# Forgetting attention in a two-block kernel: sum and row extreme in one VectorE operation, P divided on ScalarE, S5's output stored by SyncE

## The chip, the cores and the metric

The kernel runs on one core of one Trainium2 chip. Its engines are TensorE (PE in the profile), VectorE (DVE), ScalarE (ACT), GpSimd (POOL) and SyncE (SP, which issues DMAs). The metric is the device time of one execution in microseconds; three runs of the kernel before took 1682.77, 1688.86 and 1692.17 us, median 1688.86.

## What is computed

Two blocks act one after the other on x, 512 positions by 1024 channels, in float32. The first has a state-space branch, a gated linear recurrence and an attention to a memory; the second, with which the change deals, has forgetting attention (12 heads of 64), an S5 state-space layer (768 channels in 48 groups, state 64) and an attention to a memory. Cut to the two parts that matter:

```python
# forgetting attention; log_f = log_sigmoid(fl + b_forget), F = cumsum(log_f)
s = q @ k.T / sqrt(64) + F[t] - F[s]      # for s <= t, else -1e30
out = softmax(s) @ v                      # then * silu(gf)
# S5: a complex diagonal state driven by u, with a scan over the positions
h[t] = a * h[t-1] + B @ u[t];  y[t] = Re(C @ h[t]) + D * u[t]   # then gelu, gates
```

Softmax does not change when a number is added to a whole row, so the kernel leaves F[t] out and adds only -F[s].

## The kernel before

**Tiling.** The positions are 4 blocks of 128. Every matrix product is done in float32r from a high and a low part of both factors. A weight is loaded by SP in pieces of 512 KB (`wraw`, three buffers), its high part is a ScalarE copy (`whi`, L267), its low part a VectorE subtraction (`wlo`, L280), five buffers each. The unit of TensorE's main work is a *share*: half of such a job, 12 matmuls of 128x512. A job of two shares ends with an evacuation of its PSUM tile.

**Order.** All engines execute in the order in which the program is written. `lay` puts named steps between the shares by hand: in a plan string, `t12@7` puts the step t12 ahead of share 7, and steps with the same number stand in the string's order. A share itself first issues the weight splits for shares up to four ahead, then the callbacks put off with `after`, then its matmuls, then (if odd) its evacuation.

**The six turns.** `window(j, ...)` handles heads 2j and 2j+1 and one S5 block. For j below 5, its ten shares are those of the next turn's u, k, v, q and gf, in this order; the plan is `WINDOW` (L1740). The last turn has 16 shares and `LAST_WINDOW` (L1743). The steps, with a the head and tt the block of query rows:

- `s`a tt (L1679): two matmuls give the scores of 128 queries against n = 128(tt+1) keys. VectorE writes P = 0.125 scores + nb, in one operation for the n-128 earlier keys (L1691, nb = -F[s] broadcast to all partitions) and in one for the diagonal block (L1692, nbm, the same with -1e30 above the diagonal), then takes the negated row maximum (L1693). ScalarE takes the exponential with that bias and sums the rows (L1694).
- `n`a tt (L1696): VectorE takes the reciprocal of the row sums (L1699) and multiplies P (L1700).
- `t`a tt (L1702): TensorE transposes P block by block (L1708), ScalarE copies the result to SBUF (L1710). `pv` multiplies by v.
- `vt` (L1659): transposes of v, whose evacuation is L1325.
- `M0`, `M1` (L1670): for the next turn's head 0 or 1, SP loads nb (L1672) and GpSimd makes nbm (L1674).
- `nb`, `wc` (L1482, L1494): GpSimd prepares the next turn's S5 coefficients; nb ends with a sign change of 128 columns on VectorE (L1491), wc with the powers `vt` and `rho` (L1513).
- `kk`, `kt`, `tg`, `ld`, `u`: S5's kernel matrix, its copies to `Tg` by SP (L1545), the coefficients and u for the next turn, loaded by SP (L1452, L1459).
- `S`, `R`, `y`: states by matmul; the recurrence on VectorE (L1567 to L1584, reading the powers); the output by TensorE (L1592, L1596), copied by ScalarE (L1599) and stored in eight DMAs that ScalarE issues (L1601).

After the k job's evacuation, the next share splits k: ScalarE copies (L1639), VectorE subtracts (L1641), SP copies each to the other half of the partitions (L1640, L1642). In `WINDOW`, share 4 does that. The steps ahead of shares 5, 6 and 7 are nb, y; then t10, t11, n12, n13, M1; then t12, t13. Ahead of the turns, the first turn's own k, v, q, gf stand with u, `fox_nb` and `fox_vt` between them (L1768).

Of the kernel before, what the change touches and what calls it, by code (L numbers as in the profile page):

```python
# [10 lines left out]
AF = mybir.ActivationFunctionType  # L11
ALU = mybir.AluOpType
AX = mybir.AxisListType
# [6 lines left out]
EPS = 1e-6  # L20
WSPLIT = 5
NEG = -1e30


class Cols:
# [146 lines left out]
def two_blocks(ctx, tc, A, out):  # L172
    nc = tc.nc
    V, S, G, PE, SP = nc.vector, nc.scalar, nc.gpsimd, nc.tensor, nc.sync
# [51 lines left out]
    def lay(fillers, plan, steps):  # L226

        fl = []
        for f in fillers:
            fl.extend([(f, i) for i in range(len(f.parts))] if isinstance(f, Job) else [f])  # L230
        at = [(w.split("@")[0], int(w.split("@")[1])) for w in plan.split()]
        for i in range(len(fl) + 1):
            prog.extend(steps[n] for n, p in at if p == i or (i == len(fl) and p > i))
            if i < len(fl):
                prog.append(fl[i])
# [67 lines left out]
    ones = const.tile([128, 128], F32, name="ones")  # L303
# [32 lines left out]
    def ph2(name):  # L336
        o, n = P2.at[name]
        return p2[:, o:o + n]
# [17 lines left out]
    def xtile():  # L356
        return psx.tile([128, 512], F32, tag="x", name="x")
# [4 lines left out]
    def scr():  # L362
        return sp.tile([128, 512], F32, tag="t", name="t", bufs=8)

    def wide(t):
        return t.rearrange("p c h -> p (c h)")
# [110 lines left out]
    def pt(pool, tag, shape=(128, 512), dt=F32, bufs=1):  # L477
        return pools[pool + "_"].tile(list(shape), dt, tag=tag, name=tag, bufs=bufs)
# [245 lines left out]
    def q_job(j):  # L724
        def ev(ps):
            qt[j].extend(hp_tile("mrg", 2 * (j % 4) + z, F32R) for z in range(2))
            split_to(*qt[j], ps)
        return gemm(A["w_in"][WI["q"] + j], H, ev)
# [36 lines left out]
    q = [q_job(j) for j in range(8)]  # L765
# [258 lines left out]
    def ssd_step(g, what):  # L1024
# [48 lines left out]
        def l():  # L1073

            j = i
            for q_ in range(2):
                h = hs + 2 * j + q_
                M = R["M"][2 * j + q_] = pt("ssp", "M", (128, 4, 128), bufs=6)
                SP.dma_start(wide(M), acs_d[h].partition_broadcast(128))
                G.affine_select(M, M, [[0, 4], [1, 128]], ALU.is_ge, NEG, base=0, channel_multiplier=-1)  # L1080

# [237 lines left out]
    def norm2(dst, ps, scale=1.0):  # L1319

        r2 = nrm["r2"][:ps.shape[0]]
        if scale == 1.0:
            V.tensor_tensor(dst, ps, r2, ALU.mult)
        else:
            V.scalar_tensor_tensor(dst, ps, scale, r2, ALU.mult, ALU.mult)  # L1325
# [24 lines left out]
    y_d = dram.tile([768, 8, 64], F32, name="y_d")  # L1350
    s5 = {}

    def cmul(o, a, b, x, y):

        G.tensor_tensor(x, a[0], b[1], ALU.mult)
        G.tensor_tensor(y, a[1], b[1], ALU.mult)
        G.tensor_tensor(o[1], a[1], b[0], ALU.mult)
        G.tensor_tensor(o[0], a[0], b[0], ALU.mult)
        G.tensor_tensor(o[1], o[1], x, ALU.add)
        G.tensor_tensor(o[0], o[0], y, ALU.subtract)  # L1360
# [102 lines left out]
    def q4(i):  # L1463
        return s5["bc"][:, 64 * i:64 * i + 64].rearrange("p (a h) -> p a h", a=4)

    def s5_xy():
        return pt("s5p", "x"), pt("s5p", "y")
# [14 lines left out]
    def s5_nb(b):  # L1482
        def run():
            x, y = s5_xy()
            v3 = lambda t: t[:, :64].rearrange("p (a h) -> p a h", a=4)
            f3 = lambda t: t[:, 4 * b:4 * b + 4].unsqueeze(2).to_broadcast([128, 4, 16])
            bb = [pt("s5p", "bbr", (128, 64)), pt("s5p", "bbi", (128, 64))]
            cmul([v3(bb[0]), v3(bb[1])], [q4(0), q4(1)], [f3(s5["fr"]), f3(s5["fi"])], v3(x), v3(y))
            s5["NB"] = [pt("s5p", "NBr"), pt("s5p", "NBi")]
            s5_wide(s5["NB"], (v3(bb[0]), v3(bb[1])), b, slice(7, None, -1), x, y)  # L1490
            V.tensor_scalar(s5["bc"][:, 384:512], s5["bc"][:, 384:512], -1.0, None, ALU.mult)  # L1491
        return run

    def s5_wc(b):  # L1494
# [91 lines left out]
    def s5_y(b):  # L1586
        def run():
            py = xtile()
            Hb, WC, Tg, U = s5["Hb"], s5["WC"], s5["Tg"], s5["U"]
            for a in range(4):  # L1590
                for z in range(2):
                    PE.matmul(py[:, 128 * a:128 * a + 128], WC[z][:, 128 * a:128 * a + 128],  # L1592
                              Hb[z][:, a].rearrange("p z c -> p (z c)"), start=(z == 0), stop=False)
                for z in range(2):
                    g = 2 * a + z
                    PE.matmul(py[:, 64 * g:64 * g + 64], Tg[:, 128 * g:128 * g + 128], U[:, 64 * g:64 * g + 64],  # L1596
                              start=False, stop=(z == 1))
            Yt = scr()
            S.activation(Yt, py, AF.Copy)  # L1599
            for j in range(8):  # L1600
                nc.scalar.dma_start(y_d[128 * b:128 * b + 128, j, :].rearrange("(g h) c -> h g c", h=16),  # L1601
                                    Yt[16 * j:16 * j + 16].rearrange("p (g c) -> p g c", g=8))
        return run

# [3 lines left out]
    def fl_evac(ps):  # L1608

        x, a, u = scr()[:12], scr()[:12], scr()[:12]  # L1610
        V.tensor_scalar(x, ps, ph2("b_forget")[:12], -1.0, ALU.add, ALU.mult)

        def sums():
            V.tensor_tensor_scan(u, ones[:12, 0:1].to_broadcast([12, 512]), x, 0.0, ALU.mult, ALU.add)
            SP.dma_start(n_d, u)
        softplus_of(x, a, u, True, sums)

# [3 lines left out]
    def fox_tile(j, part, dt=F32):  # L1621

        i = ("q0", "q1", "k0", "k1", "kl0", "Vt", "gf", "kl1").index(part)
        return hp_tile("hhi", 4 * (j % 2) + i, dt) if i < 4 else hp_tile("acc", 4 * (j % 2) + i - 4, dt)
# [20 lines left out]
    def fox_job(j, part):  # L1645
        def ev(ps):
            if part == "gf":
                fx[j]["gf"] = fox_tile(j, "gf")
                silu2n(ps, fx[j]["gf"])
                return  # L1650
            t = scr()
            norm2(t, ps, 0.5 if part == "v" else 1.0)
            if part == "v":
                fx[j]["v"] = t
            else:
                after(1, lambda: (fox_q if part == "q" else fox_k)(j, t))
        return in2(part, j, ev)
# [11 lines left out]
    def fox_nb(j, a):  # L1669
        def run():  # L1670
            nb = pt("fxp", "nb", bufs=2)
            SP.dma_start(nb, n_d[2 * j + a].partition_broadcast(128))  # L1672
            nbm = pt("fxp", "nbm", (128, 4, 128), bufs=2)
            G.affine_select(nbm, nb.rearrange("p (c s) -> p c s", c=4), [[0, 4], [-1, 128]], ALU.is_ge, NEG,  # L1674
                            base=0, channel_multiplier=1)
            fx[j]["h"][a].update(nb=nb, nbm=nbm)
        return run

    def fox_s(j, a, tt):  # L1679
        R = fx[j]["h"][a]  # L1680
        q, k, kl = (fx[j][n][a] for n in ("q", "k", "kl"))
        n = 128 * tt + 128
        ts_ = slice(128 * tt, n)
        ps = stile()
        w = max(n, 256)
        PE.matmul(ps[:, :w], q[:, ts_], k[:, :w], start=True, stop=False)
        PE.matmul(ps[:, :w], q[:, ts_], kl[:, :w], start=False, stop=True)
        P = R["P"][tt] = pt("fxp", "P", bufs=4)
        mx = R["mx"][tt] = pt("fxp", "mx", (128, 4), bufs=6)
        if tt:  # L1690
            V.scalar_tensor_tensor(P[:, :n - 128], ps[:, :n - 128], 0.125, R["nb"][:, :n - 128], ALU.mult, ALU.add)  # L1691
        V.scalar_tensor_tensor(P[:, ts_], ps[:, ts_], 0.125, R["nbm"][:, tt], ALU.mult, ALU.add)  # L1692
        V.tensor_reduce(mx[:, 0:1], P[:, :n], AX.X, ALU.max, negate=True)  # L1693
        S.activation(P[:, :n], P[:, :n], AF.Exp, bias=mx[:, 0:1], accum_out=mx[:, 1:2])  # L1694

    def fox_n(j, a, tt):  # L1696
        P, mx = fx[j]["h"][a]["P"][tt], fx[j]["h"][a]["mx"][tt]
        n = 128 * tt + 128
        V.reciprocal(mx[:, 2:3], mx[:, 1:2])  # L1699
        V.tensor_scalar(P[:, :n], P[:, :n], mx[:, 2:3], None, ALU.mult)  # L1700

    def fox_t(j, a, tt):  # L1702
        R = fx[j]["h"][a]
# [30 lines left out]
    def th_mrg2(m):  # L1734
        def run():
# [2 lines left out]
        return run  # L1738

    WINDOW = ("s00@0 s01@0 kk@0 s02@1 s03@1 n00@1 n01@1 kt@2 tg@2 ld@2 t00@3 t01@3 s10@3 s11@3 n02@2 n03@3 S@3 R@3 M0@3 "  # L1740
              "t02@3 t03@4 s12@4 s13@4 n10@4 n11@4 nb@5 t10@6 t11@6 n12@6 n13@6 y@5 M1@6 t12@7 t13@7 vt@8 wc@8 u@8 "
              "pv@9")
    LAST_WINDOW = ("s00@0 s01@0 kk@1 s02@2 s03@2 n00@2 n01@2 kt@3 tg@3 t00@4 t01@4 s10@4 s11@4 n02@4 n03@4 S@6 R@6 "  # L1743
                   "t02@7 t03@6 s12@7 s13@7 n10@7 n11@7 t10@9 t11@9 n12@9 n13@9 y@12 t12@12 t13@12 pv@14")
# [18 lines left out]
    def fox_in(j):  # L1763
        return [fox_job(j, p) for p in ("k", "v", "q", "gf")]

    fi = fox_in(0)
    add(u_job(0), few(A["w_fl"], 12, H2, fl_evac, norm2, True))
    lay(fi, "u0@2 n0@5 v0@5 n1@6",  # L1768
        {"n0": fox_nb(0, 0), "n1": fox_nb(0, 1), "u0": s5_u(0), "v0": fox_vt(0)})
    gs = [gs_job(j) for j in range(6)]  # L1770
    gate0 = [gate2_job(0, m, th_mrg2(m)) for m in range(8)]
# [212 lines left out]
```

## Time and profile before

| | |
|---|---|
| time, median of 3 runs | 1688.86 us (1682.77 to 1692.17) |
| profiled execution | 1688.69 us, span 1687.0 us |
| granted TensorE clock, mean | 0.987 |
| TensorE matmul busy | 1630.0 us |
| VectorE, ScalarE, GpSimd busy | 1160.3, 784.7, 440.4 us |
| the six turns | from 1045 to about 1340 us |

A row of a timeline has the start, the duration, the engine, the line, the operation, what it writes and reads, and how many equal neighbours are merged in it; in brackets stands how long the engine had been idle before it, and what released it. A "q" behind an engine's name (ACTq, SPq) is its queue, which issues DMAs.

### The profile page before, as it was taken

How to read it: one execution, taken by the hardware profiler on the slowest of the kernel's cores; microseconds unless marked ns; L12 is line 12 of the kernel's file. 1: busy time of each engine (PE TensorE's matmuls, PEld its weight loads, DVE VectorE, ACT ScalarE, POOL GpSimd, SP SyncE). 2: the span in 40 equal slices, each digit the busy share in tenths (PEclk: the TensorE clock that was granted, in tenths of full speed). 3: DMA queues.
4: the chain of work that ended last, by engine and by line, in shares of the span. 5: the costliest groups of instructions: out<-in, count | busy, mean ns of one | idle time of the engine just before them, and what ended most of it. 6: DMA issues, size and time to landing. Idle time of an engine off the chain costs nothing.

```text
span 1687.0 us, 23007 instructions
## 1 busy us (share of the span) xinstructions
PE 1630.0 (97%) x8202; PEld 1333.5 (79%) x8202; DVE 1160.3 (69%) x1871; ACT 784.7 (47%) x1532; POOL 440.4 (26%) x636
## 2 busy tenths in 40 slices
PE   9999999999999999999999999998999999999998
PEld 8788887787788787878787786777787888888886
DVE  7753267768645987687767886888887545775554
ACT  6554345654543545554544654334344333544334
POOL 4200001211201422213143493665656000020002
PEclk9999999999999999999999999999999999999999
DMA  7322233243323343333432555444334323232532
GB/s 246 120 66 87 85 115 94 90 130 100 95 89 121 106 124 122 97 120 109 133 109 97 177 159 183 109 121 107 102 97 106 122 86 105 94 103 91 174 101 87
DMA packets 112834, 193.01 MB, mean 114 GB/s; under 512 B 50576, under 2 KB 57892, under 8 KB 112720
## 3 DMA queue, kind: packets, MB, share of 16 engines
q1 hardware_dynamic: 97984, 181.41, 34.5%
q10 hardware_dynamic: 14736, 10.14, 2.2%
q8 instruction: 65, 1.06, 0.3%
q14 instruction: 49, 0.40, 0.1%
HBM read 173.90 MB, written 9.54 MB: 109 GB/s over the span
## 4 chain that ended last, share of the span: by engine, by line
PE 67%; DVE 20%; ACT 5%; issue 4%; DMA 3%; POOL 0%; SPq 0%; ACTq 0%; DVEq 0%; POOLq 0%
PE g L351 47%; PE x L351 6%; DVE wlo L280 4%; PE s L351 1%; PE s L1931 1%; DMA rstd<-rs_d 1%; DVE mx L1693 1%; ACT whi L267 1%; DVE P L1700 1%; PE x L1103 1%; PE x L1720 1%; DVE acc L1641 1%; DVE ys L1137 1%; PE x L1107 1%; DVE rg L879 1%
## 5 line engine op out<-in xcount | busy, mean ns | idle before, releaser
L351 PE MATMUL g<-hlo,whi 128*128 128x512 f32 x1304 | 515.9, 396 | 0.0
L280 DVE TENSOR_TENSOR wlo<-wraw,whi 128x512 fp32r<-128x512 f32 (+1 forms) x556 | 424.8, 778 | 102.9 <-ACT whi L267 91.4
L267 ACT ACTIVATE whi<-wraw 128x512 fp32r<-128x512 f32 (+1 forms) x556 | 331.1, 607 | 234.7 <-PE g L351 98.5
L351 PE MATMUL g<-hhi,whi 128*128 128x512 f32 x832 | 331.7, 399 | 10.5 <-DVE xl L785 8.2
L351 PEld LDWEIGHTS g<-hlo,whi 128*128 128x128 f32 x1304 | 249.1, 191 | 51.0 <-issue 1.0
L351 PE MATMUL g<-hhi,wlo 128*128 128x512 f32 x832 | 224.4, 392 | 0.0
L351 PE MATMUL g<-mrg,whi 128*128 128x512 f32 x536 | 219.6, 410 | 0.0
L351 PEld LDWEIGHTS g<-hhi,whi 128*128 128x128 f32 x832 | 157.3, 189 | 47.5 <-issue 11.4
L351 PEld LDWEIGHTS g<-hhi,wlo 128*128 128x128 f32 x832 | 157.6, 189 | 33.6
L351 PE MATMUL g<-mrg,wlo 128*128 128x512 f32 x536 | 144.4, 391 | 0.0
L351 PEld LDWEIGHTS g<-mrg,whi 128*128 128x128 f32 x536 | 103.5, 193 | 22.9 <-issue 1.9
L351 PEld LDWEIGHTS g<-mrg,wlo 128*128 128x128 f32 x536 | 101.6, 190 | 22.2
L351 PE MATMUL g<-y,whi 128*128 128x512 f32 x432 | 114.2, 399 | 5.0 <-DVE t L785 2.3
L867 POOL TENSOR_TENSOR t<-la 128x512 f32<-128x512 f32 x12 | 18.2, 1514 | 321.6 <-ACT la L864 321.6
L351 PEld LDWEIGHTS g<-y,whi 128*128 128x128 f32 x432 | 79.9, 188 | 27.4 <-issue 2.7
L351 PE MATMUL x<-y,whi 128*128 128x512 f32 x336 | 85.3, 393 | 0.5 <-ACT whi L267 0.5
L785 DVE SCALAR_TENSOR_TENSOR t<-g,p,t 128x511 f32<-128x511 f32 (+2 forms) x72 | 53.9, 748 | 38.3 <-ACT t L783 36.6
L1080 POOL TENSOR_SCALAR_AFFINE_SELECT M<-M 128x512 f32<-128x512 f32 x32 | 25.5, 802 | 200.7 <-DMA M<-acs_d 94.7
L351 PEld LDWEIGHTS x<-y,whi 128*128 128x128 f32 x336 | 62.8, 188 | 14.9 <-ACT whi L267 1.3
L1859 POOL TENSOR_TENSOR hhi<-hhi,t 128x512 f32<-128x512 f32 x8 | 13.0, 1626 | 222.1 <-DVE t L1858 210.6
L351 PE MATMUL g<-y,wlo 128*128 128x512 f32 x216 | 61.4, 393 | 0.0
L1694 ACT ACTIVATE P<-P,mx 128x128 f32<-128x128 f32 (+3 forms) x48 | 27.0, 563 | 69.1 <-DVE mx L1693 66.0
(593 smaller groups left out, 2798.7 us busy)
## 6 DMA issues: line engine op xcount, KB each, us to landing
wraw<-in_w_in SPq DMA_DIRECT2D x164, 512.0 KB, 3.3
M<-acs_d SPq DMA_DIRECT2D x32, 256.0 KB, 4.5
wraw<-in_w_ssd SPq DMA_DIRECT2D x16, 512.0 KB, 3.4
wraw<-in_w_out SPq DMA_DIRECT2D x16, 512.0 KB, 3.5
wraw<-in_w_v SPq DMA_DIRECT2D x12, 512.0 KB, 3.7
wraw<-in_w_mem SPq DMA_DIRECT2D x12, 512.0 KB, 3.3
wraw<-in_w_lru SPq DMA_DIRECT2D x16, 384.0 KB, 3.0
wraw<-in_w_k SPq DMA_DIRECT2D x11, 512.0 KB, 4.8
```

The lines of the kernel that those rows point to most:

```text
L267: S.activation(hi, raw, AF.Copy)
L280: V.tensor_tensor(lo, raw, hi.bitcast(F32), ALU.subtract)
L351: PE.matmul(ps, w, X[k0 + k][low], start=(k0 + p == 0), stop=(k0 + n == nk and p == 3 * n - 1))
L785: V.scalar_tensor_tensor(dst[:, sft:], ps[:, :512 - sft], c1(cwn, (3 - sft) * nt + j), dst[:, sft:], ALU.mult, ALU.add)
L867: G.tensor_tensor(a2, a, a, ALU.mult)
L879: V.tensor_tensor(u, u, L["r"][0][j], ALU.mult)
L1080: G.affine_select(M, M, [[0, 4], [1, 128]], ALU.is_ge, NEG, base=0, channel_multiplier=-1)
L1103: PE.matmul(py[64 * q_:64 * q_ + 64, c * 128:c * 128 + 128], R["xdt"][:, c, (2 * j + q_) * 64:(2 * j + q_) * 64 + 64], M[:, c])
L1107: PE.matmul(po[:, c * 128:c * 128 + 128], R["prev"][c][:, j * 128:j * 128 + 128], R["C"][:, c * 128:c * 128 + 128])
L1137: V.scalar_tensor_tensor(y, y, c1("ssd_ng", 4 * g + i), R["rs"], ALU.mult, ALU.mult)
L1641: V.tensor_tensor(kl[a][hf], t[hf], k[a][hf].bitcast(F32), ALU.subtract)
L1694: S.activation(P[:, :n], P[:, :n], AF.Exp, bias=mx[:, 0:1], accum_out=mx[:, 1:2])
```

## The change

- The scores come negated: q is scaled by -0.125 when it is evacuated, the scan of log f subtracts, the mask is +1e30. So P holds the negated sum, and the row's minimum takes the part of the maximum. One VectorE operation adds the mask and keeps the minimum (`tensor_tensor_reduce`); for blocks after the first, the diagonal's operation starts from the minimum of the earlier keys. The exponential gets scale -1.
- P is multiplied by the reciprocal on ScalarE, and the sign change L1491 is a ScalarE copy.
- S5's output is stored by SP, in the same eight DMAs.
- n12 and n13 stand ahead of nb and y (share 5), before they stood behind t10, t11 (share 6). In the set-up, the first transposes of v stand ahead of share 7, not 5.

```diff
@@ -20,6 +20,7 @@
 EPS = 1e-6
 WSPLIT = 5
 NEG = -1e30
+BIG = 3e38
 
 
 class Cols:
@@ -1488,7 +1489,7 @@
             cmul([v3(bb[0]), v3(bb[1])], [q4(0), q4(1)], [f3(s5["fr"]), f3(s5["fi"])], v3(x), v3(y))
             s5["NB"] = [pt("s5p", "NBr"), pt("s5p", "NBi")]
             s5_wide(s5["NB"], (v3(bb[0]), v3(bb[1])), b, slice(7, None, -1), x, y)
-            V.tensor_scalar(s5["bc"][:, 384:512], s5["bc"][:, 384:512], -1.0, None, ALU.mult)
+            S.activation(s5["bc"][:, 384:512], s5["bc"][:, 384:512], AF.Copy, scale=-1.0)
         return run
 
     def s5_wc(b):
@@ -1598,7 +1599,7 @@
             Yt = scr()
             S.activation(Yt, py, AF.Copy)
             for j in range(8):
-                nc.scalar.dma_start(y_d[128 * b:128 * b + 128, j, :].rearrange("(g h) c -> h g c", h=16),
+                SP.dma_start(y_d[128 * b:128 * b + 128, j, :].rearrange("(g h) c -> h g c", h=16),
                                     Yt[16 * j:16 * j + 16].rearrange("p (g c) -> p g c", g=8))
         return run
 
@@ -1611,7 +1612,7 @@
         V.tensor_scalar(x, ps, ph2("b_forget")[:12], -1.0, ALU.add, ALU.mult)
 
         def sums():
-            V.tensor_tensor_scan(u, ones[:12, 0:1].to_broadcast([12, 512]), x, 0.0, ALU.mult, ALU.add)
+            V.tensor_tensor_scan(u, ones[:12, 0:1].to_broadcast([12, 512]), x, 0.0, ALU.mult, ALU.subtract)
             SP.dma_start(n_d, u)
         softplus_of(x, a, u, True, sums)
 
@@ -1649,7 +1650,7 @@
                 silu2n(ps, fx[j]["gf"])
                 return
             t = scr()
-            norm2(t, ps, 0.5 if part == "v" else 1.0)
+            norm2(t, ps, {"v": 0.5, "q": -0.125}.get(part, 1.0))
             if part == "v":
                 fx[j]["v"] = t
             else:
@@ -1671,7 +1672,7 @@
             nb = pt("fxp", "nb", bufs=2)
             SP.dma_start(nb, n_d[2 * j + a].partition_broadcast(128))
             nbm = pt("fxp", "nbm", (128, 4, 128), bufs=2)
-            G.affine_select(nbm, nb.rearrange("p (c s) -> p c s", c=4), [[0, 4], [-1, 128]], ALU.is_ge, NEG,
+            G.affine_select(nbm, nb.rearrange("p (c s) -> p c s", c=4), [[0, 4], [-1, 128]], ALU.is_ge, -NEG,
                             base=0, channel_multiplier=1)
             fx[j]["h"][a].update(nb=nb, nbm=nbm)
         return run
@@ -1687,17 +1688,20 @@
         PE.matmul(ps[:, :w], q[:, ts_], kl[:, :w], start=False, stop=True)
         P = R["P"][tt] = pt("fxp", "P", bufs=4)
         mx = R["mx"][tt] = pt("fxp", "mx", (128, 4), bufs=6)
-        if tt:
-            V.scalar_tensor_tensor(P[:, :n - 128], ps[:, :n - 128], 0.125, R["nb"][:, :n - 128], ALU.mult, ALU.add)
-        V.scalar_tensor_tensor(P[:, ts_], ps[:, ts_], 0.125, R["nbm"][:, tt], ALU.mult, ALU.add)
-        V.tensor_reduce(mx[:, 0:1], P[:, :n], AX.X, ALU.max, negate=True)
-        S.activation(P[:, :n], P[:, :n], AF.Exp, bias=mx[:, 0:1], accum_out=mx[:, 1:2])
+
+        lo = BIG
+        for c, m in ((slice(0, n - 128), R["nb"][:, :n - 128]), (ts_, R["nbm"][:, tt])):
+            if c.start < c.stop:
+                least = mx[:, 3:4] if c.stop < n else mx[:, 0:1]
+                V.tensor_tensor_reduce(P[:, c], ps[:, c], m, 1.0, lo, ALU.add, ALU.min, least)
+                lo = least
+        S.activation(P[:, :n], P[:, :n], AF.Exp, bias=mx[:, 0:1], scale=-1.0, accum_out=mx[:, 1:2])
 
     def fox_n(j, a, tt):
         P, mx = fx[j]["h"][a]["P"][tt], fx[j]["h"][a]["mx"][tt]
         n = 128 * tt + 128
         V.reciprocal(mx[:, 2:3], mx[:, 1:2])
-        V.tensor_scalar(P[:, :n], P[:, :n], mx[:, 2:3], None, ALU.mult)
+        S.activation(P[:, :n], P[:, :n], AF.Copy, scale=mx[:, 2:3])
 
     def fox_t(j, a, tt):
         R = fx[j]["h"][a]
@@ -1738,7 +1742,7 @@
         return run
 
     WINDOW = ("s00@0 s01@0 kk@0 s02@1 s03@1 n00@1 n01@1 kt@2 tg@2 ld@2 t00@3 t01@3 s10@3 s11@3 n02@2 n03@3 S@3 R@3 M0@3 "
-              "t02@3 t03@4 s12@4 s13@4 n10@4 n11@4 nb@5 t10@6 t11@6 n12@6 n13@6 y@5 M1@6 t12@7 t13@7 vt@8 wc@8 u@8 "
+              "t02@3 t03@4 s12@4 s13@4 n10@4 n11@4 n12@5 n13@5 nb@5 t10@6 t11@6 y@5 M1@6 t12@7 t13@7 vt@8 wc@8 u@8 "
               "pv@9")
     LAST_WINDOW = ("s00@0 s01@0 kk@1 s02@2 s03@2 n00@2 n01@2 kt@3 tg@3 t00@4 t01@4 s10@4 s11@4 n02@4 n03@4 S@6 R@6 "
                    "t02@7 t03@6 s12@7 s13@7 n10@7 n11@7 t10@9 t11@9 n12@9 n13@9 y@12 t12@12 t13@12 pv@14")
@@ -1765,7 +1769,7 @@
 
     fi = fox_in(0)
     add(u_job(0), few(A["w_fl"], 12, H2, fl_evac, norm2, True))
-    lay(fi, "u0@2 n0@5 v0@5 n1@6",
+    lay(fi, "u0@2 n0@5 n1@6 v0@7",
         {"n0": fox_nb(0, 0), "n1": fox_nb(0, 1), "u0": s5_u(0), "v0": fox_vt(0)})
     gs = [gs_job(j) for j in range(6)]
     gate0 = [gate2_job(0, m, th_mrg2(m)) for m in range(8)]
```

## Rows read from the trace of the kernel before

**Rows 1.** The page's first part: busy time of each engine, share, instructions.
```profile
PE 1630.0 (97%) x8202; PEld 1333.5 (79%) x8202; DVE 1160.3 (69%) x1871; ACT 784.7 (47%) x1532; POOL 440.4 (26%) x636
```

**Rows 2.** Busy time in a stretch: length, five engines, PEclk, DMA share, GB/s.
```profile
1103.60:1151.40 47.80, 43.70 (x290) 36.36 (x290) 40.27 (x84) 18.76 (x43) 30.83 (x60) 0.96 0.40 108
```

**Rows 3.** The waits from 1020 to 1340 us: total, times, longest.
```profile
PE s L1708 <- DVE mx L1699: 17.1, 6, 4.6
PE s L1708 <- DVE P L1700: 2.8, 4, 0.9
PE s L1663 <- DVE t L1325: 2.8, 1, 2.8
```

**Rows 4.** TensorE's timeline, the third turn's wait.
```profile
1175.38 1.68 PE L1708 MATMUL s<-ident,P 128*128 128x128 f32 x7 [4.56 <-DVE mx L1699]
```

**Rows 5.** The 5 us after that wait, columns as in rows 2.
```profile
1175.00:1180.00 5.00, 4.57 (x17) 3.72 (x18) 2.43 (x5) 2.88 (x8) 4.24 (x4) 0.66 0.55 155
```

**Rows 6.** VectorE's timeline ahead of the third turn's last block of P.
```profile
1168.19 3.02 DVE L1641 TENSOR_TENSOR acc<-t,hhi 64x512 fp32r<-64x512 f32 x2
...
1175.34 0.48 DVE L1700 TENSOR_SCALAR P<-P,mx 128x512 f32<-128x512 f32 x1
```

**Rows 7.** Instructions by line: ns minimum/median/maximum, first and last start, forms.
```profile
L1691 DVE SCALAR_TENSOR_TENSOR P<-s,nb x36: 280/413/548, 1046.5 to 1313.8; 128x128 f32<-128x128 f32 x12, 128x256 f32<-128x256 f32 x12, 128x384 f32<-128x384 f32 x12
L1692 DVE SCALAR_TENSOR_TENSOR P<-s,nbm x48: 272/280/292, 1045.9 to 1314.3; 128x128 f32<-128x128 f32 x48
L1693 DVE TENSOR_REDUCE mx<-P x48: 285/487/689, 1046.2 to 1314.6; 128x1 f32<-128x128 f32 x12, 128x1 f32<-128x256 f32 x12, 128x1 f32<-128x384 f32 x12, 128x1 f32<-128x512 f32 x12
L1700 DVE TENSOR_SCALAR P<-P,mx x48: 285/421/1310, 1053.4 to 1318.6; 128x128 f32<-128x128 f32 x12, 128x256 f32<-128x256 f32 x12, 128x384 f32<-128x384 f32 x12, 128x512 f32<-128x512 f32 x12
L1491 DVE TENSOR_SCALAR bc<-bc x6: 293/980/1174, 966.6 to 1265.5; 128x128 f32<-128x128 f32 x6
```

**Rows 8.** ScalarE's timeline in the third turn, and its copy L1710 by line.
```profile
1165.07 0.73 ACT L1694 ACTIVATE P<-P,mx 128x512 f32<-128x512 f32 x1 [0.68 <-DVE mx L1699]
...
1167.61 0.60 ACT L1599 ACTIVATE t<-x 128x512 f32<-128x512 f32 x1
1168.24 6.46 ACTq L1601 DMA_DIRECT2D y_d<-t  x8
1174.75 0.63 ACT L267 ACTIVATE whi<-wraw 128x512 fp32r<-128x512 f32 x1 [6.54 <-DMA y_d<-t]
...
L1710 ACT ACTIVATE PT<-s x48: 255/423/608, 1056.8 to 1334.3; 128x128 f32<-128x128 f32 x12, 128x256 f32<-128x256 f32 x12, 128x384 f32<-128x384 f32 x12, 128x512 f32<-128x512 f32 x12
```

**Rows 9.** SP's issues in the third turn, and ScalarE's store issues by line.
```profile
1172.20 0.33 SPq L1672 DMA_DIRECT2D nb<-n_d  x1
...
1176.88 3.70 SPq L1459 DMA_DIRECT2D U<-u_d  x8
...
L1601 ACTq DMA_DIRECT2D y_d<-t x48: 309/444/1537, 1072.6 to 1333.4; - x48
```

**Rows 10.** Timelines from mask to powers to R to y, and y's first and fifth.
```profile
1175.76 1.16 POOL L1674 TENSOR_SCALAR_AFFINE_SELECT nbm<-nb 128x512 f32<-128x512 f32 x1 [2.20 <-DMA nb<-n_d]
1195.96 0.11 POOL L1513 MEMSET rho<- 128x4 f32 x1
1203.27 0.41 DVE L1567 TENSOR_TENSOR x<-x,vtr 128x252 f32<-128x252 f32 x1
...
1154.89 0.41 DVE L1567 TENSOR_TENSOR x<-x,vtr 128x252 f32<-128x252 f32 x1
1160.74 0.42 DVE L1584 SCALAR_TENSOR_TENSOR Hb<-y 64x256 f32<-64x256 f32 x1
1161.19 0.39 PE L1592 MATMUL x<-Hb,WCr 128*128 128x128 f32 x2
...
1065.51 0.39 PE L1592 MATMUL x<-Hb,WCr 128*128 128x128 f32 x2
1257.04 0.39 PE L1592 MATMUL x<-Hb,WCr 128*128 128x128 f32 x2
```

## The prediction

> **What bounds the kernel now.** I read the page's first part, then the windows by stage, the waits of the stretch with the changed lines, and then each engine's timeline there. TensorE is busy for 97% of the span [rows 1], so an edit on another engine pays only where TensorE stands still. The changed lines run from about 1033 to 1334 us, in six turns (one per pair of heads, called windows in the code), of which the first five are alike. A turn lasts some 47.9 us, TensorE is busy for 43.7 of a stretch that long, and its mean granted clock there is 0.96 [rows 2]. Nearly all of the missing time has one cause: the transposes of P (L1708) wait 17.1 us for "mx L1699" and 2.8 us for "P L1700", and the transposes of v (L1663) 2.8 us for the evacuation L1325 [rows 3]. It is one wait per turn, such as the 4.56 us of the third [rows 4]. All but about 0.3 us of the 19.9 us lies in the first five turns: 3.9 us each. After such a wait the granted clock was 0.66 over the next 5 us, that is the 1.2 GHz level for some two thirds of them, which costs (1 - 0.66) x 5 = 1.7 us [rows 5]. So a turn loses about 5.6 us, and the wait on v, at the same price, 2.8 + 1.7 = 4.5 us. Full cover for all is 5 x 5.6 + 4.5 + 0.3 = 32.8 us.
>
> Why P is late: VectorE is in order. In front of P's last two normalisations stand the subtractions of the key split (3.02 us for two), the sign change L1491 and, behind these, a weight's low part and v's evacuation; P's last row block is divided only at 1175.34 us [rows 6]. ScalarE is blocked as well: eight store issues hold its queue for 6.46 us, and the weight copy behind them has waited 6.54 us [rows 8].
>
> **The change, part by part.**
>
> *Scores.* Per tile, a sum into P (two for all but the first tile) and a maximum become one or two sums that keep the minimum. What goes is L1693, 48 x 0.29 to 0.69 us, 0.49 at the median [rows 7], about 3.9 us of VectorE per turn. The new operation isn't in this trace. Low end: what L1691 and L1692 take with the same operands, 0.28 to 0.55 us; under that I see no way, since the same elements are read from PSUM. High end: sum plus maximum, so that nothing is saved. I take the low end, the rows nearest to it: one pass over the same data. The high end would add about 1.5 us for the two long tiles of a turn's second head. The scale of -0.125 moves into q's evacuation, which has the form of v's, and the scan and the mask change a sign: nothing.
>
> *Normalisation on ScalarE.* L1700 goes (48 x 0.29 to 1.31 us, median 0.42 [rows 7]), and so does L1491 (0.98 at the median). ScalarE gets 48 scaled copies. Low end: its copies L1710 of these sizes, 0.26 to 0.61 us; high end: the exponential, 0.73 us at 512 columns [rows 8]. I take 0.5 and 0.6 us for the two long ones. ScalarE is 47% busy [rows 1] and loses the store issues, so this is nothing by itself. It is an ordering cost: each copy waits for its reciprocal on VectorE, with all of ScalarE behind it.
>
> A point on the port. L1700 and L1491 stretch to 1.31 and 1.17 us when GpSimd works, while the sums from PSUM stay within 0.27 to 0.29 and 0.28 to 0.55 us [rows 7]. The Trainium skill, "SBUF — State Buffer", on the shared port pair, says that GpSimd locks out a VectorE operation in a two-port mode or with two SBUF inputs; the new sum reads one input from PSUM. By that rule it would not be held up, and its price stays at the low end; the trace agrees for the old sums.
>
> *Order.* The reciprocals of the last two blocks move ahead of the output y and of the weight split of the next share. With 2 maxima, 2 normalisations, L1491, one weight split and v's evacuation gone from in front, P is ready some 4 to 5 us before the 1175.4 us at which the transposes now start, about when TensorE arrives. The wait at L1708 goes in all five turns. In the first set-up, v's transposes stand two shares later, so the wait of 2.8 us goes; what is late next there, the query split and the mask, is wanted only in the first turn.
>
> *The stores on SP: what comes late next.* y's copy Yt (L1599) and its eight stores are now in a longer chain. In program order SP has the key copies, then the stores, and behind them the load of the bias row for the next turn's second head (L1672); on GpSimd the mask (L1674) waits for that load, and behind the mask stands the whole preparation of the state's powers, which ends with L1513 and which the next turn's recurrence R (L1567) reads. R's last operation ends at 1161.16 us, y starts at 1161.19 us [rows 10]: y has no slack against R. Today that preparation ends at 1196.07 us and R begins at 1203.27 us, 7.2 us of slack, of which 6.3 us is that turn's wait with its clock, which is to go.
>
> The new loop from R to R, each step from the third turn:
> - R itself: 1154.89 to 1161.16 us, 6.3 us [rows 10].
> - From R's end to the end of the key's subtractions: 1161.16 to 1171.2 us today, 10.0 us [rows 6, 10]. Two maxima and two normalisations go, about 2.7 us; but the key's copies on ScalarE get two normalisations in front of them, so I count 1.5 us: 8.5 us.
> - Reciprocals 0.2, two normalisations 1.1, the moved L1491 0.3 and Yt 0.6 us [rows 8]: 2.2 us. Today Yt does not wait for the reciprocals (1167.61 us); now it ends near 1171.9 us.
> - Eight stores on SP: eight loads of the mirrored shape take 3.70 us there; the same stores take 6.46 us on ScalarE's queue [rows 8, 9]. I take 4.4 us, nearer to SP's own row.
> - L1672 to mask: 1172.20 to 1175.76 us, 3.6 us [rows 9, 10].
> - Mask to the last operation of the powers: 1175.76 to 1196.07 us, 20.3 us, and 0.1 us to R [rows 10].
>
> Sum: 45.4 us. TensorE's own turn without the wait is 47.9 - 5.6 = 42.3 us, so the loop sets the end: y would wait about 3 us per turn, from the second turn to the fifth. Of the 5.6 us some 2.5 are kept.
>
> By the Trainium skill, "DMA: Bandwidth & Descriptors", section "Issuing engines are not separate DMA queues", a change of the issuing engine saves only issue time. By that the transfers stay as they are, and what moves is the line on SP.
>
> **The sum.** The first y starts at 1065.51 us, the fifth at 1257.04 us [rows 10]: 191.5 us, which become 4 x 45.4 = 181.6: 9.9 us. The fifth turn's wait lies behind the last of them, and the sixth turn needs its powers far later: 5.6 us. Set-up 4.5 us, the last turn's small waits 0.3 us. Together 20.3 us. The profiled execution took 1688.69 us, 1687.0 of span and 1.7 around it, and the median of the runs is 1688.86: **1668 us**. Behind 1334 us nothing changes but that y's stores are issued by SP in the sixth turn too, among weight loads that are issued several shares early.
>
> **The rivals.**
> 1. *The loop closes in time, all of the waits go.* For it: fewer VectorE operations beside GpSimd, which stretch its powers too; the second step could shrink by the full 2.7 us. Against it: it needs 3 us. 1688.7 - 32.8 = 1656 us. Chance 0.20.
> 2. *The loop is longer*: stores at ScalarE's 6.46 us, or sums at their high end: 47 to 48.5 us, a gain of 14 down to 8 us: 1675 to 1681 us. Chance 0.16.
> 3. *No change*: both of these and a later landing, a loop of 48.5 to 52.5 us. What is won at the transposes is lost at y; left are the set-up and the fifth turn, less what the loop adds: 1681 to 1697 us. Chance 0.12.
> 4. *Slower*: SP's issues are as long as the longest of the ScalarE ones, 1.54 us [rows 9]: 8 x 1.54 = 12.3 us, 7.9 more than I count, a loop of 53.3 us. Four loops are 213.2 us, 21.7 more than today; less 10.4 that is won outside, 11 us slower: 1700 us. It decides from a loop of 52.6 us on. Against it: SP's loads show 0.46 us each. Chance 0.07.
> That the waits at L1708 stay is not likely: four things in front of them go.
>
> **How the numbers follow.** The forecast (loops of 44 to 47 us, 1662 to 1675 us) has 0.45. The range goes from rival 1, a few us under it for the scatter of the runs, to the end of rival 2: 1653 to 1682 us. No change is within 0.5%, 8.4 us, which is about what can be told here. Faster takes the forecast and rivals 1 and 2: 0.45 + 0.20 + 0.16 = 0.81; same is rival 3, 0.12; slower rival 4, 0.07.
>
> **What would show it.** Right: no wait at L1708 in the five turns, but one at L1592 of 2 to 4 us in turns two to five, with VectorE's L1567 waiting for GpSimd, GpSimd idle for some us in front of the second L1674 of a turn, and 45.4 us from y to y. The set-up's wait at L1663 is gone. Wrong: no wait at L1592 (rival 1), sums over 0.7 us at 384 columns, stores on SP over 0.8 us each, or L1708 still waiting, now for ScalarE.

## The result and the profile after

The changed kernel takes 1661.0 us, the median of four runs (1657.83 to 1662.57); the kernel before 1686.68 us, also of four runs (1682.77 to 1692.17). The ratio is 0.9843, with a 95% interval of 0.9809 to 0.9877: 20.7 to 32.2 us faster. The forecast was 1668 us in a range of 1653 to 1682; the time lies 1 us under the band of 1662 to 1675 us in which the prediction put its main case. The profiled execution took 1657.83 us with a span of 1656.1.

Lines up to about L1690 are one higher than before; the new sum is L1696, the reciprocal L1703, P's normalisation L1704, its transposes L1712, the copies of these L1714. In the experiments each row has the line numbers of its own run.

The page's first part, which answers to [rows 1]:

```profile
PE 1617.7 (98%) x8202; PEld 1325.4 (80%) x8202; DVE 1115.9 (67%) x1853; ACT 806.4 (49%) x1586; POOL 435.9 (26%) x636
```

TensorE's busy time falls by 12.3 us and its share rises by one hundredth; where the 30.9 us between the two spans are doesn't show in such shares. TensorE's waits from 1020 to 1340 us tell more (waiter and its line, releaser; total, times, longest). This is all of TensorE's part of the answer, where [rows 3] had 22.7 us in three rows:

```profile
PE x L1593 <- DVE Hb L1584: 5.7, 4, 2.1
```

No transpose waits for P or for v any more. In their place stands one new wait, S5's output y for the recurrence R. TensorE's timeline at the first y of each of the five alike turns, answering to [rows 10]:

```profile
1057.27 0.39 PE L1593 MATMUL x<-Hb,WCr 128*128 128x128 f32 x2
...
1100.11 0.46 PE L1593 MATMUL x<-Hb,WCr 128*128 128x128 f32 x2 [0.83 <-DVE Hb L1584]
...
1144.49 0.46 PE L1593 MATMUL x<-Hb,WCr 128*128 128x128 f32 x2 [2.08 <-DVE Hb L1584]
...
1188.25 0.46 PE L1593 MATMUL x<-Hb,WCr 128*128 128x128 f32 x2 [1.26 <-DVE Hb L1584]
...
1232.29 0.46 PE L1593 MATMUL x<-Hb,WCr 128*128 128x128 f32 x2 [1.56 <-DVE Hb L1584]
```

The first turn has no wait and the next four have one each: a loop that goes once around per turn. Four turns take 1232.29 - 1057.27 = 175.0 us, 43.76 us each, against 191.5 us before.

Where the 30.9 us are. The first matmul of a group well ahead of the change, L938, starts at 1013.29 us before, and the same matmul after (L939) at 1009.43: 3.9 us lie in code that is alike in both, so they are scatter of this pair of executions. From there to the first y 52.2 us became 47.8, a gain of 4.4. From the first y to the fifth, 16.5. From the fifth y to the end, 430.0 us became 423.8, 6.2. The changed stretch thus gave 27.1 us.

The loop of the third turn, on VectorE, ScalarE, SP and GpSimd in turn (SP's rows are issues):

```profile
1138.42 0.41 DVE L1568 TENSOR_TENSOR x<-x,vtr 128x252 f32<-128x252 f32 x1 [0.33 <-PE g L352]
...
1144.26 0.42 DVE L1585 SCALAR_TENSOR_TENSOR Hb<-y 64x256 f32<-64x256 f32 x1
...
1150.28 2.84 DVE L1642 TENSOR_TENSOR acc<-t,hhi 64x512 fp32r<-64x512 f32 x2 [1.13 <-ACT hhi L1640]
1153.15 0.22 DVE L1703 RECIPROCAL mx<-mx 128x1 f32<-128x1 f32 x2
```

```profile
1153.41 1.23 ACT L1704 ACTIVATE P<-P,mx 128x384 f32<-128x384 f32 x2 [2.51 <-DVE mx L1703]
1154.55 0.29 ACT L1492 ACTIVATE bc<-bc 128x128 f32<-128x128 f32 x1
1154.75 0.57 ACT L1600 ACTIVATE t<-x 128x512 f32<-128x512 f32 x1
```

```profile
1155.35 3.67 SPq L1602 DMA_DIRECT2D y_d<-t  x8
1159.06 0.43 SPq L1673 DMA_DIRECT2D nb<-n_d  x1
```

```profile
1163.45 0.63 POOL L1675 TENSOR_SCALAR_AFFINE_SELECT nbm<-nb 128x512 f32<-128x512 f32 x1 [7.47 <-DMA nb<-n_d]
...
1182.41 0.10 POOL L1514 MEMSET rho<- 128x4 f32 x1
```

```profile
1181.78 0.06 DVE L1566 MEMSET x<- 128x4 f32 x1 [2.22 <-POOL vti L1360]
1182.18 0.41 DVE L1568 TENSOR_TENSOR x<-x,vtr 128x252 f32<-128x252 f32 x1 [0.33 <-issue]
```

The next R starts at 1182.18 us, which is 43.76 us after 1138.42. Each step begins where the one ahead of it has let it go. ScalarE stood idle for 2.51 us in front of the normalisation, and GpSimd for 7.47 us in front of the mask. VectorE's wait for the powers lies ahead of the two small clears (L1566) that stand in front of R's first product (L1568). In the waits of VectorE from 1020 to 1340 us it is this row, one wait in each of the turns two to five:

```profile
DVE x L1566 <- POOL vti L1360: 9.6, 4, 3.0
```

### The profile page after: what moved, and what is told of

The parts are those of the page before. It is cut to its first block, busy times and chain, and to the rows that moved or that the text cites. A ratio compares the mean times of both kernels' runs of the same rounds, so it can differ in the third digit from the quotient of the medians.

```text
span 1656.1 us, 23097 instructions
## 1 busy us (share of the span) xinstructions
PE 1617.7 (98%) x8202; PEld 1325.4 (80%) x8202; DVE 1115.9 (67%) x1853; ACT 806.4 (49%) x1586; POOL 435.9 (26%) x636
## 4 chain that ended last, share of the span: by engine, by line
PE 68%; DVE 16%; ACT 4%; POOL 4%; DMA 4%; issue 3%; SPq 1%; DVEq 0%; ACTq 0%; POOLq 0%
PE g L352 48%; PE x L352 7%; DVE wlo L281 4%; PE s L352 1%; PE s L1935 1%; DMA rstd<-rs_d 1%; PE x L1104 1%; DMA nb<-n_d 1%; ACT whi L268 1%; DVE ys L1138 1%; PE x L1108 1%; DVE y L389 1%; DVE rg L880 1%; PE s L345 1%; DVE xl L786 1%
## 5 line engine op out<-in xcount | busy, mean ns | idle before, releaser
L352 PE MATMUL g<-hlo,whi 128*128 128x512 f32 x1304 | 510.1, 391 | 0.0
L352 PEld LDWEIGHTS g<-hlo,whi 128*128 128x128 f32 x1304 | 245.6, 188 | 50.0 <-issue 1.0
L352 PE MATMUL g<-mrg,whi 128*128 128x512 f32 x536 | 214.5, 400 | 0.0
L868 POOL TENSOR_TENSOR t<-la 128x512 f32<-128x512 f32 x12 | 18.2, 1513 | 319.6 <-ACT la L865 319.6
```

The costliest lines, as they stand in the source:

```text
L352: PE.matmul(ps, w, X[k0 + k][low], start=(k0 + p == 0), stop=(k0 + n == nk and p == 3 * n - 1))
L868: G.tensor_tensor(a2, a, a, ALU.mult)
```

## The experiments

Each ratio is against the kernel before, with its 95% interval. "Turn" is the mean of the four stretches from y to y. The theory is the prediction's: the loop R, key split, normalisations, Yt, stores, bias load, mask, powers, R sets the turn in the changed kernel, and TensorE's own work does so when the loop is shorter. Against it stood that the new wait was only the old one moved, with VectorE's or ScalarE's work as the bound.

**The bias load ahead of the stores.**

```
- WINDOW: ... t10@6 t11@6 y@5 M1@6 t12@7 ...
+ WINDOW: ... t10@6 t11@6 M1@5 y@5 t12@7 ...
```

> The changed kernel, with the load of the bias row for the next turn's second head (step M1) put ahead of y and its stores. Loop theory (the time from y to y is set by the stores on SP, the load behind them, the mask and the powers on GpSimd, and R): eight stores of 3.7 us leave the loop of 43.8 us, 40.1 is less than TensorE's own 42.3, so the wait of TensorE for Hb in turns two to five (0.8 to 2.1 us, 5.7 in all) goes, y to y is 42.3 us, and the time falls by about 6 us against the changed kernel (near 1655 us median, 0.981 of before). Rival theory (R is late because VectorE's own queue is long): the wait stays at 1 to 2 us, y to y 43.8 us, no change in time.

1653.55 us, ratio 0.9798 [0.9782, 0.9814]. The turn is 41.85 us, and y waits in no turn. All of TensorE's waiting in the stretch is this one row of the waits:

```profile
PE x L1597 <- DMA Tg<-KR: 0.5, 1, 0.5
```

On SP the bias load now goes first, and the same eight stores take the same time behind it:

```profile
1150.11 0.58 SPq L1673 DMA_DIRECT2D nb<-n_d  x1
...
1151.80 3.70 SPq L1602 DMA_DIRECT2D y_d<-t  x8
```

No instruction was removed, only the order on SP changed (GpSimd's is the same in both runs), and 7.4 us went, which is 4 x (43.76 - 41.85) = 7.6. That the loop runs through the stores and the load behind them is shown.

**The stores twice.**

```
+ for j in range(8):
+     SP.dma_start(y_e[...], Yt[16 * j:16 * j + 16]...)   # a scratch tensor
  for j in range(8):
      SP.dma_start(y_d[...], Yt[16 * j:16 * j + 16]...)
```

> The changed kernel, with eight further stores of the same tile to a second scratch tensor ahead of y's own stores on SP. Loop theory: 8 x 0.46 = 3.7 us more in the loop, 47.4 us from y to y, a wait for Hb at y of 3.5 us or more with the granted clock at its lower level behind it; four turns cost 4 x 3.7 = 14.6 us: 1675 us. Rival theory (SP's queue has slack, y waits for something else): no change.

1680.65 us, 0.996 [0.9943, 0.9977]. The turn is 48.05 us, 4.3 more than the changed kernel's; the eight stores had taken 3.67. The time is 5.7 us over the 1675 us that I expected: the four turns give 17.2 us instead of 14.6, and from the fifth y to the sixth it is 65.0 us against 62.3. The same wait grew, and with it came the clock. TensorE's timeline at the second y, and the 5 us behind it (columns as in [rows 2]):

```profile
1108.51 0.77 PE L1594 MATMUL x<-Hb,WCr 128*128 128x128 f32 x2 [5.19 <-DVE Hb L1585]
...
1108.50:1113.50 5.00, 4.99 (x24) 5.00 (x24) 3.76 (x14) 2.48 (x7) 4.92 (x9) 0.50 0.03 7
```

**The stores back on ScalarE.**

```
- SP.dma_start(y_d[...], Yt[...])
+ nc.scalar.dma_start(y_d[...], Yt[...])
```

> The changed kernel, with S5's output stored by ScalarE again. Loop theory: the load behind the stores on SP is free of them, so the wait for Hb at y goes as in the run with M1 first; but ScalarE's queue is held for about 6 us between Yt and the copies of the transposed P, so that PV, which wants the last of them, waits up to 3 us: y to y between 42.3 and 45 us, time within 6 us of the changed kernel to either side. Rival theory (moving the stores to SP is what freed the transposes at L1712): the wait at the transposes comes back with some 4 us per turn and y to y is about 47 us. If the stores had no part in the loop: wait for Hb at y unchanged.

1666.63 us, 0.9871 [0.9851, 0.989]. The wait at y goes, as SP's line is short again, but another takes its place, v's transposes for the copies of P on ScalarE:

```profile
PE s L1664 <- ACT PT L1714: 9.2, 5, 2.6
```

ScalarE's timeline in the third turn says why:

```profile
1160.75 3.83 ACTq L1602 DMA_DIRECT2D y_d<-t  x8
...
1165.16 0.53 ACT L1714 ACTIVATE PT<-s 128x128 f32<-128x128 f32 x2
1166.11 0.98 ACT L1714 ACTIVATE PT<-s 128x384 f32<-128x384 f32 x2
```

I expected P's product to be late; it was the transposes of v ahead of it. The issues take about as long on one engine as on the other here (3.83 and 3.67 us); what differs is who stands behind them. The turn is 43.73 us, as in the changed kernel; from the fifth y to the sixth it takes 66.0 us against 62.3, which is 3.7 of the 5.6 us between the two medians. There lies the longest of the five waits, 2.57 us, with a granted clock of 0.66 over the 5 us behind it. The rest is about what two such medians scatter. So from the first y to the fifth the stores on SP gain nothing in this order: one wait went, one of the same size came.

**The normalisation back on VectorE.**

```
- S.activation(P[:, :n], P[:, :n], AF.Copy, scale=mx[:, 2:3])
+ V.tensor_scalar(P[:, :n], P[:, :n], mx[:, 2:3], None, ALU.mult)
```

> The changed kernel, with P multiplied by the reciprocals on VectorE again (the order and the rest as changed). Loop theory: Yt no longer stands behind normalisations on ScalarE (2.2 us go from the loop), the key's copies on ScalarE are freed of two more, VectorE gets four operations of some 0.5 us back between R and the last block of P: the loop is 1 to 2 us shorter, 42 to 43 us, so the wait for Hb at y is under 0.7 us; the last blocks of P are ready up to 1.5 us later than TensorE. y to y 42 to 43.5 us, time between 5 us under the changed kernel and equal. Rival theory (the move to ScalarE is what freed the transposes): their wait is back with 3 to 4.5 us, y to y 46 to 48 us, 10 to 20 us above the changed kernel.

1655.4 us, 0.982 [0.9801, 0.9838]: 5.6 us faster than the changed kernel. The turn is 42.38 us, and y does not wait; one wait of 0.9 us for P is left at the transposes. ScalarE copies Yt without waiting for the reciprocals:

```profile
1148.81 0.58 ACT L1600 ACTIVATE t<-x 128x512 f32<-128x512 f32 x1
```

That is 5.97 us behind the third turn's y (1142.84 us). In the changed kernel this copy came at 1154.75 us, 10.26 us behind its y, after the 2.51 us in which ScalarE waited for L1703. So the move to ScalarE, in this order of the program, costs.

**Both of them: bias load first, normalisation on VectorE.** The two edits above together.

> The changed kernel with M1 ahead of y and P multiplied on VectorE. Loop theory: with M1 ahead, TensorE's own turn (41.85 us, as measured with M1 first alone) is the bound, and both places of the multiplication fit under it; the last blocks of P come up to 1 us later than with ScalarE, so at most one wait of that size in some turns: y to y 41.9 to 42.6 us, time equal to the run with M1 first within 4 us. Rival theory (the multiplication on ScalarE costs by itself, not through the loop): faster than the run with M1 first by some 5 us.

1653.49 us, 0.9798 [0.978, 0.9817], turn 42.1 us: the same as with the bias load alone. TensorE's own work is the end of what this stretch can give by order.

**The old order of n12 and n13.**

```
- WINDOW: ... n10@4 n11@4 n12@5 n13@5 nb@5 t10@6 t11@6 y@5 M1@6 ...
+ WINDOW: ... n10@4 n11@4 nb@5 t10@6 t11@6 n12@6 n13@6 y@5 M1@6 ...
```

> The changed kernel, with the steps n12 and n13 back behind t10 and t11. Loop theory: Yt no longer stands behind two normalisations that wait for their reciprocals (2.5 us of waiting and 1.2 of work), so the loop is some 3 us shorter and the wait for Hb at y goes or is under 1 us; P of the last two blocks is ready later, so 1 to 2 us of wait come back at the transposes; y to y 43 to 45 us, time within 5 us of the changed kernel. Rival theory (the order is what removes the wait at the transposes): that wait comes back with 3 to 4.5 us and its clock loss of 1.7, y to y 46 to 48 us, time 10 to 20 us above the changed kernel.

1659.84 us, 0.9833 [0.9816, 0.9851], the same as the changed kernel; the turn is 43.39 us. One wait was exchanged for another of the same size:

```profile
PE s L1712 <- ACT P L1704: 5.3, 5, 1.2
```

**The order alone, in the kernel before.** n12 and n13 moved as the change does, nothing else.

> The kernel before, with only n12 and n13 moved ahead of nb and y. Theory of the sum of parts: VectorE still has the maxima and the multiplications, so the wait at the transposes shrinks by the two operations no longer in front (L1491, a weight's low part and v's evacuation, some 3 us, less what y's own order adds): 1 to 2.5 us of wait are left per turn, y to y 45 to 47 us, time 5 to 14 us under before. Rival theory (the order alone does it): no wait, y to y 42.3 us, time some 28 us under before.

1678.27 us, 0.9947 [0.993, 0.9964], some 9 us less (0.0053 of 1687); the turn is 45.85 us. The waits at L1708 are 11.1 us in five rows instead of 19.9 in two, three waits of some 0.6 us for the recurrence come at y, and the set-up's 2.8 us at L1663 stay.

**The new scores alone, in the kernel before.** The sums, q's scale, the scan and the mask as in the change, nothing else.

> The kernel before, with the new scores alone (negated, sum and minimum in one operation). Queue theory (VectorE's line in front of P's last blocks): from R on two minima of 0.56 and 0.69 us go, and R itself starts up to 0.7 us earlier, so the wait at the transposes shrinks from 3.9 to about 2 us and its clock loss may stay: y to y 45.5 to 46.5 us, time 7 to 12 us under before. Rival theory (the maxima ran beside the wait for something else): time unchanged.

1674.09 us, 0.993 [0.9904, 0.9955], some 12 us less (0.007 of 1686), turn 45.08 us. That mean is of three turns of 43.9 to 44.6 us and one of 48.0, with a wait of 3.2 us in it and a granted clock of 0.50 over the 5 us behind. The waits (a fourth row has 0.6 us):

```profile
PE s L1712 <- DVE mx L1703: 6.3, 5, 3.2
PE s L1712 <- DVE P L1704: 3.4, 4, 0.9
PE s L1664 <- DVE t L1326: 2.8, 1, 2.8
```

**The old scores in the changed kernel.** The sum and the minimum as two operations again:

```
- V.tensor_tensor_reduce(P[:, c], ps[:, c], m, 1.0, lo, ALU.add, ALU.min, least)
+ V.scalar_tensor_tensor(P[:, c], ps[:, c], 1.0, m, ALU.mult, ALU.add)
+ V.tensor_reduce(mx[:, 0:1], P[:, :n], AX.X, ALU.min)   # once, behind the sums
```

> The changed kernel, with the sum and the row minimum as separate VectorE operations again (two sums and one minimum per tile). Loop theory: the minima of the two long tiles of the second head come back into the loop, 0.56 + 0.69 us less the accumulator reads, 1 to 1.5 us: loop 45 us, wait for Hb at y 2 to 3.5 us, time 4 to 7 us above the changed kernel. Rival theory (VectorE is not on the loop, ScalarE's queue sets it): y to y 43.8 us and no change in time.

1665.49 us, 0.9877 [0.9862, 0.9893], 4.5 us slower than the changed kernel, and the turn is 44.75 us, both as expected. The waits are not: I had put 2 to 3.5 us at y, and y waits 1.1 to 1.7 us while P's transposes wait as well:

```profile
PE x L1593 <- DVE Hb L1584: 5.7, 4, 1.7
PE s L1711 <- ACT P L1703: 2.9, 4, 1.0
```

The scores give some 12 us alone and 4.5 us on top of the rest: the parts overlap, since each takes something out of the same stretch ahead of P.

**The normalisation alone, in the kernel before.** L1700 as a ScalarE copy, nothing else.

> The kernel before, with the multiplication of P by the reciprocals on ScalarE alone. Queue theory: in this order the last two multiplications stand behind the eight stores that hold ScalarE for 6.5 us, two weight copies and the copies of the first transposes, so that they begin near 1176.5 us of the third turn where VectorE ended them at 1175.8: the wait at the transposes grows by 1 to 2 us, y to y 48.5 to 50 us, time 3 to 10 us above before. Rival theory (a VectorE operation less in front is a gain): 2 to 7 us under before.

1687.32 us, 1.0003 [0.9992, 1.0014]: no change, and I had expected it to be slower. The wait changed its owner and kept its size:

```profile
PE s L1708 <- ACT P L1700: 20.8, 6, 4.3
```

ScalarE's timeline in the third turn: the store issues stand ahead of the normalisation, but took 4.74 us instead of the 6.46 us of [rows 8]:

```profile
1167.12 4.74 ACTq L1601 DMA_DIRECT2D y_d<-t  x8
...
1172.86 1.23 ACT L1700 ACTIVATE P<-P,mx 128x384 f32<-128x384 f32 x2
```

P's longest block ends at 1174.09 us there, 14.2 us behind the third turn's y at 1159.90; in the kernel before it ended at 1175.82 [rows 6], 14.6 us behind its y [rows 10]. I had put ScalarE's queue at its old length. The same shows in every run with the stores on ScalarE: in the five alike turns the eight issues took 5.6 to 8.2 us in the three with P's multiplication on VectorE (the kernel before, the order alone, the scores alone), and 3.8 to 5.0 us in the two with it on ScalarE. Why is open.

**The set-up's old order.**

```
- lay(fi, "u0@2 n0@5 n1@6 v0@7", ...)
+ lay(fi, "u0@2 n0@5 v0@5 n1@6", ...)
```

> The changed kernel, with v's first transposes ahead of share 5 again in the set-up. Theory: a wait of TensorE of about 2.8 us at them and a granted clock under 1 behind it, together 4 to 4.5 us more between the start of the second block and the first y; nothing else changes. Rival theory: v's evacuation is early enough now that VectorE has less to do: no wait.

The wait for v's evacuation is back:

```profile
1036.09 1.12 PE L1664 MATMUL s<-ident,t 128*128 128x128 f32 x4 [2.74 <-DVE t L1326]
```

From the matmul L939 to the first y it takes 51.8 us, 4.0 more than the changed kernel's 47.8. The single time, 1668.65 us, is 10.8 us over the changed kernel's profiled execution. Of these 5.2 us lie ahead of L939, in code that is alike in both, so they are scatter; 4.0 us are the set-up's, and 1.6 us come in the turns (44.16 us each), one of which has a wait of 2.90 us at y.

## Why the prediction was right, and the term that was off

*The waits that go, and the one that comes* were forecast in their place. L1708 and L1663 wait no more; y waits from the second turn to the fifth, released by the recurrence. The bias load's move shows that it is the loop and not VectorE's load by itself: it took the wait away without one operation less.

*The sum, term by term*, from the two profiled executions:

| term | forecast | measured |
|---|---|---|
| set-up | 4.5 | 4.4 (4.0 when undone alone) |
| first y to fifth y | 9.9 | 16.5 |
| behind the fifth y | 5.6 + 0.3 | 6.2 |
| together | 20.3 | 27.1 |

The second is the mis-sized term: its mechanism was right, the loop was put at 45.4 us and is 43.76. Its own steps, against the forecast in the order in which the prediction has them:

| step | forecast | measured, third turn |
|---|---|---|
| R | 6.3 | 6.3 |
| R's end to the end of the key's subtractions | 8.5 | 8.4 |
| reciprocals, normalisations, L1492, Yt | 2.2 | 2.2 |
| eight stores | 4.4 | 3.7 |
| bias load to mask | 3.6 | 4.4 |
| mask to the next R | 20.3 + 0.1 | 18.7 |
| sum | 45.4 | 43.8 (rounded steps: 43.7) |

The stores are SP's own 3.70 us [rows 9], and I had gone 0.7 above it; the load landed 0.8 us later behind them, so these two cancel. What is left is the last step, 1.7 us, which I had carried over as it was. Some 0.4 of it is that R starts on the last powers that it reads (L1361, which ended at 1182.13 us) and not on L1514's end: R began at 1182.18 us, and L1514 ended at 1182.51. The other 1.25 us is that GpSimd's chain itself got shorter. From the start of the mask to the end of the powers it takes, turn by turn:

| run | chain starts behind y, us | chain in the five turns, us |
|---|---|---|
| stores on ScalarE | 11.5 to 13.0 | 20.4, 20.5, 20.7, 20.4, 20.8 |
| bias load first | 12.6 to 15.7 | 20.7, 20.3, 20.3, 20.3, 20.9 |
| kernel before | 13.4 to 14.6 | 20.2, 20.5, 20.3, 20.2, 20.8 |
| normalisation back on VectorE | 15.8 to 17.4 | 20.1, 20.3, 20.0, 20.3, 19.8 |
| changed kernel | 18.1 to 19.7 | 19.0, 18.9, 19.1, 18.9, 19.8 |
| old scores | 19.7 to 21.1 | 18.8, 18.8, 18.8, 18.8, 19.9 |
| stores twice | 23.0 to 24.6 | 18.0, 18.1, 18.2, 18.2, 20.0 |

The first two and the last run have P's multiplication on ScalarE, as the changed kernel has, and differ from it only in the stores or the bias load; what these edits do to the chain is to start it earlier or later. So it is its place in the turn that sets its length, by what VectorE does beside it. That P's multiplication left VectorE is not what shortened the chain from the kernel before: no multiplication starts inside it there, in any of the five turns. With the normalisation back on VectorE four multiplications lie beside the third turn's chain, 1.7 us in all; what they add there is not separated from the earlier start. What does run beside it are the subtractions `wlo` and `hhi`, which read both inputs from SBUF: in the third turn seven in the kernel before and with the bias load first, four in the changed kernel, three with the stores twice, for chains of 20.3, 20.3, 19.1 and 18.2 us. In the fifth turn, which the longer last turn follows, six lie beside it in the changed kernel and with the stores twice, for 19.8 and 20.0 us. The third turn's chain with the bias load first:

```profile
1156.36 0.62 POOL L1675 TENSOR_SCALAR_AFFINE_SELECT nbm<-nb 128x512 f32<-128x512 f32 x1
...
1176.59 0.10 POOL L1514 MEMSET rho<- 128x4 f32 x1
```

Their number is not the whole of it: with the normalisation alone moved, in the kernel before, seven of them lie beside a chain of 19.4 us, and why is open. The Trainium skill, "SBUF — State Buffer", section "SBUF: two separate sides", says that the two engines share a port pair which one instruction holds whole, and that a VectorE operation in a two-port mode, or with two SBUF inputs, contends for it; the trace agrees for these subtractions, by the counts and lengths just given. The prediction had said with rival 1 that fewer VectorE operations beside GpSimd could shorten the powers, but not that the loop, by starting the chain later, would bring that about by itself.

*The clock.* I priced a wait with the clock behind it, 1.7 us for a 4.56 us wait [rows 5]. That holds for the stores issued twice, 0.50 to 0.66 behind waits of 3.0 to 5.2 us. Behind the waits at y in the changed kernel it does not arise. The 5 us after the longest:

```profile
1144.90:1149.90 5.00, 5.00 (x38) 4.61 (x38) 4.18 (x13) 2.91 (x8) 4.65 (x9) 1.00 0.01 3
```

The granted clock is 1.00, the 2.4 GHz level, behind each of the four. TensorE's own turn was put at 42.3 us, its measured value is 41.85, so the loop cost 1.9 us a turn, where I had said about 3, and the waits at y are 0.8 to 2.1 us, where I had looked for 2 to 4.

*The new operation* has the low price that I took. By line:

```profile
L1696 DVE CUSTOM_DVE_ANT_0 P<-s,nb x36: 278/414/556, 1037.9 to 1283.5; 128x128 f32<-128x128 f32 x12, 128x256 f32<-128x256 f32 x12, 128x384 f32<-128x384 f32 x12
L1696 DVE CUSTOM_DVE_ANT_0 P<-s,nbm,mx x36: 349/351/353, 1038.2 to 1284.1; 128x128 f32<-128x128 f32 x36
L1696 DVE DVE_READ_ACCUMULATOR2_ANT mx<- x84: 75/82/85, 1037.9 to 1284.4; 128x1 f32 x84
```

The sum with a minimum costs what the sum alone did [rows 7], 0.07 us more when it starts from another minimum (0.351 against 0.280), and 0.08 for reading the minimum out.

*What was right for the total but not for the part.* The prediction costed the normalisation on ScalarE as an ordering cost and put 0.5 and 0.6 us on it; it earned nothing alone, and in the changed kernel it costs 5.6 us, as it puts the reciprocals' wait ahead of Yt, the stores and the bias load. Rival 1, the loop closing in time, failed in the change by 1.9 us a turn, and came true with the bias load ahead of the stores: 1653.55 us where it had 1656.

## What to carry to other kernels

After a wait is taken away, follow what each queue has in front of the next wait, across the turn's end, and do not carry a step's length over as fixed when the loop moves it to another place in the turn: the loop over SP's stores, a load, a mask and GpSimd's powers ran over four engines and had no wait on TensorE before. In a queue, put the load that a long chain begins with ahead of stores that nobody waits for; here that was worth 7.4 us without an instruction less. Moving an operation to a less busy engine also gives it a place in that engine's order, and everything behind it then waits for its inputs: count that, not its duration.

## What the runs showed of the hardware

A VectorE sum with a running minimum takes the time of the sum alone, as above. Of TensorE's waits from 1020 to 1340 us, in all of these runs, those of 2.5 to 5.2 us were followed by 5 us at a granted clock of 0.50 to 0.71, but for one: 2.61 us, with the order alone, and 1.00 behind it. Those of 1.0 to 2.1 us were followed by 1.00, but for two: 1.53 us at y with the old scores (0.68), and 1.41 us with a further 0.89 us right behind it with the order alone (0.66). So the length of a wait does not by itself say what clock follows it. The same GpSimd chain took 18.0 to 20.9 us in the runs of the table above, by where in the turn it ran. The eight loads of u that stand behind the stores on SP took 6.41 us to issue in the third turn (from 1160.07 us), where the kernel before took 3.70 us [rows 9]; nothing waited for them.
